# An encoder trunk on one core: the weights' sums of the FFN's block products made by adding transfers, the other sums on VectorE

## The chip, the cores and the metric

The kernel runs on one core of one Trainium2 chip. Its engines are called as in the profile: PE (TensorE matmul; PEld is its weight load), DVE (VectorE), ACT (ScalarE), POOL (GpSimd) and SP (SyncE, which only issues transfers here). The metric is the device time of one execution in microseconds, the median of three runs.

## The reference, cut to what matters

Two layers over 1024 tokens of width 1024 in float32: windowed attention in the first, a gated linear recurrence in the second, each with cross-attention into 256 memory tokens. Each layer ends with a gated FFN of width 2816 (22 blocks of 128) with a convolution of three taps along the tokens.

```python
def conv_ffn(v, w_in, conv_w, conv_b, w_out):
    gate, up = jnp.split(v @ w_in, 2, axis=-1)
    hid = jax.nn.gelu(dwconv_centred(gate, conv_w, conv_b)) * up
    return hid @ w_out
...
        h = h + rmsnorm(y, norm_g[layer, 1])
        f = conv_ffn(rmsnorm(h, norm_g[layer, 2]), ffn_w_in[layer], ffn_conv_w[layer],
                     ffn_conv_b[layer], ffn_w_out[layer])
        h = h + rmsnorm(f, norm_g[layer, 3])
```

## The kernel before

**Arithmetic.** Every float32 operand is split into two float32r parts, a high part that ACT casts and a low part, the remainder, that DVE subtracts (`split`, L83 to L85; the same in `wunit`, L73 to L75). A product is three matmuls: high by high, high by low, low by high (`mmk`, L496).

**The program.** `start` (memory keys and values, and the norm of the eight token tiles, interleaved), `window` (attention of layer 0), `WOut.finish`, `ffn` of layer 0, `hgrn`, `WOut.finish` and `ffn` of layer 1, in this order. A norm takes its reciprocal root from POOL (`rstd_of`, L91: nrs, prs), and in the attention POOL adds the two halves of the rotary embedding (L247 and L248: rq from t1 and t2), which PE then transposes (L256: ptq).

**The FFN's block products.** `ffn` (L499) multiplies 2 x 2 blocks with seven products instead of eight, by sums of operand blocks. The blocks of the first matmul are halves of the contraction, gate against up, and halves of the tokens. Its first two units (`PLAIN`) are done plainly; `operands` makes the sums of the activations meanwhile, on DVE. Then 20 units of one block of 128 hidden columns follow:

- `load` fetches the unit's weights on SP, two units ahead.
- `weights` makes four sums of 128x512 (L605, L606, L608, L612) and seven splits of 512 wide, one product's operand each. They are drawn one by one between the products of the unit before (`ahead`).
- `prod` runs a product of 12 matmuls into one of the PSUM banks X, V or Y. Between products ACT or DVE reads the partial sums out (s1, s5, su, g, u).
- `conv` does the convolution, gelu and gate: two operations of ACT and three of DVE, 1024 wide (L536 to L541).
- `hidden` makes, for each pair of units, four sums of the hidden activations of 128x512 on POOL (L655 to L658: tt) and stores seven blocks to DRAM (hd).
- `sums`, for each pair of units, loads the four weight blocks of the second matmul (L635: w), adds four times on POOL (L637 to L640) and stores the sums to DRAM (w2s).

The second half of the FFN is seven products over the tokens and 11 pairs of hidden blocks each (`SECOND`, 132 matmuls a product). `unit` loads a weight block and a hidden block and splits them. The last product (k = 4) keeps its last `LAST` pairs back and runs them token tile by token tile; after each comes `tail`: the norm, the residual, the store and, in layer 0, the norm and transposes of the next layer (`norm_T`). The other four tiles have their `tail` within the same product, after its pairs 1, 3, 5 and 7.

**What sets the order.** The lines above do not. A scheduler with a simulated timeline puts each instruction in its engine's queue as early as its model has it ready, so that work of the FFN can stand far ahead of its place in the code. Each engine's queue then runs strictly in that order. A transfer also waits for the semaphore slot that the transfer eight before it on the same kind of queue used.

Of the kernel before, what the change touches and what calls it, by code (L numbers as in the profile page):

```python
# [39 lines left out]
LAST = 3  # L40
# [4 lines left out]
def build(tc, A, out):  # L45
# [59 lines left out]
    def norm_T(pl, pst, src, g, dh, dl, t, tag="n"):  # L105
        ss = pl.tile([P, 1], F32, tag=tag + "ss", name=tag + "ss")
        u = pl.tile([P, D], F32, tag=tag + "u", name=tag + "u")
        sumsq(pl, src, ss, u)
        rs = rstd_of(pl, ss, 1, D, tag)
        dve.scalar_tensor_tensor(u, src, rs[:, 0:1], g, op0=ALU.mult, op1=ALU.mult)  # L110
        for b in range(2):
            ps = pst.tile([P, 4, P], F32, tag="pt", name="pt")
            for k in range(4):
                pe.transpose(ps[:, k, :], u[:, (4 * b + k) * P:(4 * b + k + 1) * P], ident)  # L114
            split(dh[:, 4 * b:4 * b + 4, t * P:(t + 1) * P],
                  dl[:, 4 * b:4 * b + 4, t * P:(t + 1) * P], ps)
# [224 lines left out]
    class WOut:  # L341
# [84 lines left out]
        def finish(self):  # L426
# [28 lines left out]
            self.first = wunit(A["ffw1"][l, 0, :, 1024:], pl=self.wf) if l == 0 else None  # L455
# [43 lines left out]
    def ffn(l, wo, dst, gnext, halves_, out_halves):  # L499
# [13 lines left out]
        ORDER = (1, 5, 6, 2, 7, 3, 4)  # L513
# [4 lines left out]
        half = [None, 0]  # L518

        def slot():  # L520

            if half[1] == 0:
                half[0] = [ring.tile([P, 1024], F32R, tag=t, name=t) for t in ("wh", "wl")]
            c = slice(half[1] * 512, (half[1] + 1) * 512)
            half[1] = 1 - half[1]
            return half[0][0][:, c], half[0][1][:, c]

# [5 lines left out]
        def conv(f, g, ups):  # L533
# [6 lines left out]
            for m, u in ups:  # L540
                dve.tensor_tensor(c[:, m], u, c[:, m], op=ALU.mult)  # L541
# [5 lines left out]
        def plain(f):  # L547

            wg = wo.first if f == 0 and wo.first else wunit(A["ffw1"][l, f, :, 1024:])
            wu = wunit(A["ffw1"][l, f, :, :1024])  # L550
# [6 lines left out]
            for ps, m in ((gi, ti), (gj, tj)):  # L557
                act.activation(g[:, m], ps, AF.Copy, scale=-1.0)
            return conv(f, g, ((ti, ui), (tj, uj)))

        def operands():
# [3 lines left out]
            for kk in range(2):  # L565
# [12 lines left out]
                t3, t2, t4 = tmp("w2"), tmp("c", 3), tmp("sx")  # L578
# [11 lines left out]
        def load(f):  # L590
            raw = [stg.tile([P, 1024], F32, tag="st", name="st") for _ in range(2)]
            for x, r in enumerate(raw):
                nc.sync.dma_start(r, A["ffw1"][l, f, :, x * 1024:(x + 1) * 1024])
            return raw

        def weights(raw):

            a1, a2 = raw
            L_, R_ = slice(0, 512), slice(512, 1024)
            sx = fp.tile([P, 1024], F32, tag="sx", bufs=1, name="sx")  # L600
            def op(src, neg=False):
# [4 lines left out]
            dve.tensor_tensor(sx[:, R_], a2[:, L_], a2[:, R_], op=ALU.add)  # L606
# [21 lines left out]
        w2d = dram.tile([NP2, P, 4, 512], F32, name=f"w2s{l}")  # L628
        even = [None]

        def sums(p):

            r = fp.tile([P, 4, 512], F32, tag="w2", bufs=1, name="w2")
            s3 = fp.tile([P, 512], F32, tag="s3", bufs=1, name="s3")
            nc.sync.dma_start(r, A["ffw2"][l, p])  # L635
            a11, a12, a21, a22 = (r[:, q, :] for q in range(4))
            pool.tensor_tensor(s3, a11, a21, op=ALU.add)  # L637
            pool.tensor_tensor(a21, a21, a22, op=ALU.add)  # L638
# [23 lines left out]
        def first_units():  # L662
# [10 lines left out]
            ops = [next(gen) for _ in range(7)]  # L673
# [3 lines left out]
            def start(w):  # L677

                prod(1, w, X[-1], True)
                s[1] = fp.tile([P, 512], F32, tag="s1", bufs=1, name="s1")  # L680
                act.copy(s[1], X[-1])
# [600 lines left out]
```

## Time and profile before

| | before |
|---|---|
| median of 3 runs | 2832.14 us (2828.93 to 2833.56) |
| the profiled execution | 2830.25 us, its span 2828.4 us |
| mean granted clock of TensorE | 0.977 |
| transfers | 355.12 MB, 126 GB/s over the span |

Five stages follow one another; the two FFNs take from about 596 to 1270 us and from 2137 us to the end. Times of rows are microseconds from the span's start unless marked as durations. In a row of a group, the numbers behind the bar are the busy time in us, the mean duration of one in ns, and the idle time of the engine just before them with what ended it. PE's clock is granted by a throttle, and a row of busy time by stretches shows it as a share of full speed.

### The profile page before, as it was taken

Reading aid. Unit: us, or ns where it says so; the run is one execution under the profiler, and the core shown is the slowest. Engines: PE = TensorE matmul, PEld = TensorE weight load, DVE = VectorE, ACT = ScalarE, POOL = GpSimd, SP = SyncE. Lnnn points to the kernel's source line nnn. Section 1 sums busy time; section 2 is a strip of 40 time slices with the busy share of each in tenths; the row PEclk is TensorE's granted clock in tenths of the full one; section 3 lists DMA queues with packets and bytes.
Section 4 is the critical chain, followed back from the end, with each engine's and each line's share of the span. In section 5 each row is a group of like instructions: output and inputs, shape, how many; then the busy total and the mean of one; then the engine's idle time right before and its main releaser. Section 6 shows DMA issues by size and latency. Waiting matters only on the chain.

```text
span 2828.4 us, 38853 instructions
## 1 busy us (share of the span) xinstructions
PE 2687.6 (95%) x14264; PEld 2286.9 (81%) x14264; DVE 1987.3 (70%) x3227; ACT 1376.0 (49%) x2614; POOL 641.1 (23%) x525
## 2 busy tenths in 40 slices
PE   8999989997899999997999999999898899999998
PEld 7888877886778888887898888898787777888886
DVE  6588676678876765575757778878477886776555
ACT  6367676534334444454544545545454334444443
POOL 1210120215531110021112223222212553111012
PEclk9999999998999999998999999999999899999999
DMA  7111213734553336672111111111562564323766
GB/s 280 52 42 29 60 57 99 233 120 168 199 180 105 104 119 234 193 245 92 42 53 46 46 34 49 40 41 60 155 203 94 190 229 154 112 97 133 224 193 216
DMA packets 182127, 355.12 MB, mean 126 GB/s; under 512 B 16816, under 2 KB 73520, under 8 KB 179120
## 3 DMA queue, kind: packets, MB, share of 16 engines
q1 hardware_dynamic: 179488, 348.18, 37.3%
q10 hardware_dynamic: 2448, 4.46, 0.4%
q8 instruction: 112, 1.84, 0.3%
q14 instruction: 79, 0.65, 0.1%
HBM read 257.68 MB, written 94.90 MB: 125 GB/s over the span
## 4 chain that ended last, share of the span: by engine, by line
PE 76%; DVE 9%; POOL 5%; issue 4%; DMA 3%; ACT 2%; SPq 0%; DVEq 0%; POOLq 0%; ACTq 0%
PE X L496 19%; PE V L496 12%; PE pj L79 7%; PE pj L80 7%; PE pj L81 7%; PE pb L80 3%; PE pb L79 3%; PE pb L81 3%; PE Y L496 3%; PE po L1100 1%; PE pt L308 1%; PE pa L1052 1%; DMA w<-in_ffw_dram 1%; PE pt L114 1%; POOL w L638 1%
## 5 line engine op out<-in xcount | busy, mean ns | idle before, releaser
L85 DVE TENSOR_TENSOR wl<-st,wh 128x512 fp32r<-128x512 f32 (+1 forms) x314 | 322.3, 1040 | 228.8 <-ACT wh L84 224.9
L84 ACT CAST wh<-st 128x512 fp32r<-128x512 f32 (+1 forms) x314 | 246.9, 800 | 305.4 <-PE X L496 126.4
L79 PE MATMUL pj<-wh,uh 128*128 128x256 f32 (+1 forms) x768 | 235.7, 307 | 1.0 <-DVE ul L85 0.5
L81 PE MATMUL pj<-wh,ul 128*128 128x256 f32 (+1 forms) x768 | 234.2, 305 | 0.0
L80 PE MATMUL pj<-wl,uh 128*128 128x256 f32 (+1 forms) x768 | 233.9, 305 | 0.0
L79 PE MATMUL pj<-uh,wh 128*128 128x512 f32 x512 | 205.1, 401 | 4.8 <-DVE xl L85 2.5
L80 PE MATMUL pj<-ul,wh 128*128 128x512 f32 x512 | 203.9, 398 | 0.0
L81 PE MATMUL pj<-uh,wl 128*128 128x512 f32 x512 | 203.2, 397 | 0.0
L75 DVE TENSOR_TENSOR wl<-st,wh 128x1024 fp32r<-128x1024 f32 (+1 forms) x93 | 119.1, 1287 | 46.4 <-ACT wh L74 46.2
L79 PEld LDWEIGHTS pj<-wh,uh 128*128 128x128 f32 x768 | 147.7, 192 | 3.0 <-DVE ul L85 0.9
L80 PEld LDWEIGHTS pj<-wl,uh 128*128 128x128 f32 x768 | 147.8, 193 | 1.1
L81 PEld LDWEIGHTS pj<-wh,ul 128*128 128x128 f32 x768 | 147.6, 192 | 0.5
L1046 POOL TENSOR_TENSOR E<-EP,q 128x256 f32<-128x256 f32 x64 | 51.3, 801 | 414.5 <-DVE EP L1039 386.0
L74 ACT CAST wh<-st 128x1024 fp32r<-128x1024 f32 (+1 forms) x103 | 104.0, 1016 | 79.7 <-PE pj L80 42.8
L496 PE MATMUL V<-uh,wh 128*128 128x512 f32 x344 | 135.5, 394 | 4.5 <-ACT wh L84 4.5
L496 PE MATMUL V<-uh,wl 128*128 128x512 f32 x344 | 135.7, 394 | 3.4 <-DVE wl L85 3.4
L496 PE MATMUL X<-wh,wl 128*128 128x512 f32 x352 | 137.0, 390 | 0.0
L496 PE MATMUL X<-wl,wh 128*128 128x512 f32 x352 | 136.8, 389 | 0.0
L496 PE MATMUL X<-wh 128*128 128x512 f32 x352 | 136.4, 389 | 0.0
L496 PE MATMUL V<-ul,wh 128*128 128x512 f32 x344 | 135.3, 393 | 0.0
L79 PEld LDWEIGHTS pj<-uh,wh 128*128 128x128 f32 x512 | 96.8, 189 | 24.0 <-DVE xl L85 2.9
L81 PEld LDWEIGHTS pj<-uh,wl 128*128 128x128 f32 x512 | 96.8, 189 | 19.8
(365 smaller groups left out, 7813.8 us busy)
## 6 DMA issues: line engine op xcount, KB each, us to landing
st<-in_ffw_dram SPq DMA_DIRECT2D x88, 512.0 KB, 4.2
st<-hid SPq DMA_DIRECT2D x154, 256.0 KB, 4.2
w<-in_ffw_dram SPq DMA_DIRECT2D x22, 1024.0 KB, 5.0
hid<-tt SPq DMA_DIRECT2D x88, 256.0 KB, 2.1
st<-w2s SPq DMA_DIRECT2D x88, 256.0 KB, 4.0
w2s<-w SPq DMA_DIRECT2D x22, 768.0 KB, 3.3
hid<-c SPq DMA_DIRECT2D x66, 256.0 KB, 2.5
st<-in_ffw_dram SPq DMA_DIRECT2D x66, 256.0 KB, 3.8
```

The costliest lines, as they stand in the source:

```text
L74: act.copy(h[:, :n], raw)
L75: (eng or dve).tensor_tensor(l[:, :n], raw, h[:, :n].bitcast(F32), op=ALU.subtract)
L79: pe.matmul(o, ah, bh, start=first, stop=False)
L80: pe.matmul(o, ah, bl, start=False, stop=False)
L81: pe.matmul(o, al, bh, start=False, stop=last)
L84: act.copy(h, src)
L85: dve.tensor_tensor(l, src, h.bitcast(F32), op=ALU.subtract)
L114: pe.transpose(ps[:, k, :], u[:, (4 * b + k) * P:(4 * b + k + 1) * P], ident)
L308: pe.transpose(tp[:, j, :], sm[:, j, c * P:(c + 1) * P], ident)
L496: pe.matmul(o, x, y, start=new, stop=e, skip_group_check=not first)
L638: pool.tensor_tensor(a21, a21, a22, op=ALU.add)
L1046: pool.tensor_tensor(gl, pl_, ql, op=ALU.mult)
```

## The change

Four things are done.

1. The sums of the first matmul's weights: `load` fetches blocks into two more tiles (sx, sy) and adds to them by three transfers that POOL issues with `accum_op` (the sum of source and destination is written to the destination). `weights` only splits: three operands of 1024, two products' each, and one of 512. The order of the products becomes 2, 5, 6, 7, 3, the next unit's 1, and 4, and ACT copies g and, in the plain units, u out of PSUM.
2. The sums of the second matmul's weights: `sums` makes them inside DRAM by six transfers of POOL, three copies and three that add.
3. The four sums in `hidden` move from POOL to DVE.
4. The second half: the first four tails move from the last product to the one before (k = 2), with the transposes kept for the last; `LAST` is 7 in layer 0 and 10 in layer 1, and a new pool holds 5 and 8 of those operands.

The weight arrays are laid out to match. The core of the diff:

```diff
-LAST = 3
+LAST = (7, 10)
+HOLD = (5, 8)
...
-    def norm_T(pl, pst, src, g, dh, dl, t, tag="n"):
+    def norm_T(pl, pst, src, g, dh, dl, t, tag="n", ub=2, halt=False):
...
-        u = pl.tile([P, D], F32, tag=tag + "u", name=tag + "u")
+        u = pl.tile([P, D], F32, tag=tag + "u", bufs=ub, name=tag + "u")
...
+        def turn(pst):
+            for b in range(2):
...
+        if halt:
+            return turn
+        turn(pst)
...
-            for ps, m in ((gi, ti), (gj, tj)):
-                act.activation(g[:, m], ps, AF.Copy, scale=-1.0)
-            return conv(f, g, ((ti, ui), (tj, uj)))
+            u = fp.tile([P, T], F32, tag="u", bufs=1, name="u")
+            for gp, up_, m in ((gi, ui, ti), (gj, uj, tj)):
+                act.activation(g[:, m], gp, AF.Copy, scale=-1.0)
+                act.copy(u[:, m], up_)
+            return conv(f, g, u)
...
-                t3, t2, t4 = tmp("w2"), tmp("c", 3), tmp("sx")
+                t3, t2, t4 = tmp("sy", 2), tmp("c", 3), tmp("sx", 2)
...
         def load(f):
-            raw = [stg.tile([P, 1024], F32, tag="st", name="st") for _ in range(2)]
-            for x, r in enumerate(raw):
-                nc.sync.dma_start(r, A["ffw1"][l, f, :, x * 1024:(x + 1) * 1024])
-            return raw
+            w = A["ffw1"][l, f]
+            a1 = stg.tile([P, 1024], F32, tag="st", name="st")
+            a22 = stg.tile([P, 1024], F32, tag="st", name="st")[:, :512]
+            sx, sy = [fp.tile([P, 1024], F32, tag=t, bufs=2, name=t) for t in ("sx", "sy")]
+            nc.sync.dma_start(a1, w[:, 1024:])
+            for c in range(2):
+                nc.sync.dma_start(sx[:, c * 512:(c + 1) * 512], w[:, :512])
+            nc.sync.dma_start(sy, w[:, 1024:])
+            nc.sync.dma_start(a22, w[:, 512:1024])
+            pool.dma_start(sx, w[:, 512:1536], accum_op=ALU.add, max_dma_last_dim=8192)
+            pool.dma_start(sy[:, :512], sx[:, :512], accum_op=ALU.add, max_dma_last_dim=8192)
+            pool.dma_start(sy[:, 512:], sy[:, :512], accum_op=ALU.add, max_dma_last_dim=8192)
+            return a1, sx, sy, a22
         def weights(raw):
-            a1, a2 = raw
-            L_, R_ = slice(0, 512), slice(512, 1024)
-            sx = fp.tile([P, 1024], F32, tag="sx", bufs=1, name="sx")
-            def op(src, neg=False):
-                h, l_ = slot()
-                (nsplit if neg else split)(h, l_, src)
-                return h, l_
-            dve.tensor_tensor(sx[:, L_], a1[:, L_], a2[:, L_], op=ALU.add)
-            dve.tensor_tensor(sx[:, R_], a2[:, L_], a2[:, R_], op=ALU.add)
-            yield op(a1[:, L_])
-            dve.tensor_tensor(a1[:, L_], sx[:, R_], a1[:, L_], op=ALU.add)
-            yield op(sx[:, R_])
-            yield op(a1[:, L_])
-            s4 = fp.tile([P, 512], F32, tag="s4", bufs=1, name="s4")
-            dve.tensor_tensor(s4, a1[:, L_], a1[:, R_], op=ALU.add)
-            yield op(a1[:, R_])
-            yield op(sx[:, L_])
-            yield op(s4)
-            yield op(a2[:, R_])
+            for src in raw:
+                n = src.shape[-1]
+                h, l_ = [ring.tile([P, 1024], F32R, tag=t, name=t)[:, :n] for t in ("wh", "wl")]
+                split(h, l_, src)
+                yield h, l_
+        def operand(units, k):
+            u, c = {1: (0, 0), 2: (0, 1), 5: (1, 0), 7: (1, 1), 6: (2, 0), 3: (2, 1), 4: (3, 0)}[k]
+            return tuple(x[:, c * 512:(c + 1) * 512] for x in units[u])
...
-        w2d = dram.tile([NP2, P, 4, 512], F32, name=f"w2s{l}")
...
         def sums(p):
-            r = fp.tile([P, 4, 512], F32, tag="w2", bufs=1, name="w2")
-            s3 = fp.tile([P, 512], F32, tag="s3", bufs=1, name="s3")
-            nc.sync.dma_start(r, A["ffw2"][l, p])
-            a11, a12, a21, a22 = (r[:, q, :] for q in range(4))
-            pool.tensor_tensor(s3, a11, a21, op=ALU.add)
-            pool.tensor_tensor(a21, a21, a22, op=ALU.add)
-            pool.tensor_tensor(a11, a11, a21, op=ALU.add)
-            pool.tensor_tensor(a12, a12, a11, op=ALU.add)
-            nc.sync.dma_start(w2d[p][:, 0:3, :], r[:, 0:3, :])
-            nc.sync.dma_start(w2d[p][:, 3, :], s3)
+            w, o = A["ffw2"][l, p], w2d[p]
+            for c in range(2):
+                pool.dma_start(o[c], w[0])
+            pool.dma_start(o[2:4], w[2:4])
+            pool.dma_start(o[0:2], w[1:3], accum_op=ALU.add, max_dma_last_dim=8192)
+            pool.dma_start(o[2], o[0], accum_op=ALU.add, max_dma_last_dim=8192)
+            pool.dma_start(o[3], o[2], accum_op=ALU.add, max_dma_last_dim=8192)
...
-            pool.tensor_tensor(t1[:, lo], e[:, oi], e[:, oj], op=ALU.subtract)
-            pool.tensor_tensor(t1[:, hi], c[:, oj], e[:, oj], op=ALU.subtract)
-            pool.tensor_tensor(t2[:, lo], t1[:, hi], e[:, oi], op=ALU.add)
-            pool.tensor_tensor(t2[:, hi], t2[:, lo], c[:, oi], op=ALU.subtract)
+            dve.tensor_tensor(t1[:, lo], e[:, oi], e[:, oj], op=ALU.subtract)
+            dve.tensor_tensor(t1[:, hi], c[:, oj], e[:, oj], op=ALU.subtract)
+            dve.tensor_tensor(t2[:, lo], t1[:, hi], e[:, oi], op=ALU.add)
+            dve.tensor_tensor(t2[:, hi], t2[:, lo], c[:, oi], op=ALU.subtract)
...
-                w = dict(zip(ORDER, ops))
-                ahead()
-                prod(5, w[5], v, True)
-                s5 = fp.tile([P, 512], F32, tag="s5", bufs=1, name="s5")
-                act.copy(s5, v)
-                ahead()
-                prod(6, w[6], x, False)
-                su = fp.tile([P, 512], F32, tag="su", bufs=1, name="su")
-                act.copy(su, x)
-                ahead()
-                prod(2, w[2], y, True)
+                w = lambda k: operand(ops, k)
+                prod(2, w(2), y, True)
                 u = fp.tile([P, T], F32, tag="u", bufs=1, name="u")
                 dve.tensor_tensor(u[:, ti], y, s[1], op=ALU.add)
                 ahead()
-                prod(7, w[7], x, False)
+                prod(5, w(5), v, True)
+                s5 = fp.tile([P, 512], F32, tag="s5", bufs=1, name="s5")
+                act.copy(s5, v)
+                prod(6, w(6), x, False)
+                su = fp.tile([P, 512], F32, tag="su", bufs=1, name="su")
+                act.copy(su, x)
+                prod(7, w(7), x, False)
                 g = gtile()
-                dve.tensor_tensor(g[:, tj], x, s5, op=ALU.add)
+                act.copy(g[:, tj], x)
+                dve.tensor_tensor(g[:, tj], g[:, tj], s5, op=ALU.add)
                 ahead()
...
-            h, l_ = [ring.tile([P, 1024], F32R, tag=t, name=t) for t in ("wh", "wl")]
+            pl = hold_pool if k == 4 and 0 <= p - (NP2 - LAST[l]) < HOLD[l] else ring
+            h, l_ = [pl.tile([P, 1024], F32R, tag=t, name=t) for t in ("wh", "wl")]
...
-            if todo and len(made) < 3:
+            if todo and len(made) < (LAST[l] if todo[0][0] == 4 else 3):
...
+        hold_pool = tc.alloc_tile_pool(name=f"fh{l}", bufs=HOLD[l], reuse_waits="tile")
...
-                norm_T(np_, pst, x, g0, uh, ul, 4 * b + t)
+                return norm_T(np_, pst, x, g0, uh, ul, 4 * b + t, ub=4, halt=True)
...
-                if k == 4 and p in (1, 3, 5, 7):
-                    t = p // 2
-                    tail(ib, t, y["c12"][:, t, :], ss["q12"][:, t:t + 1], y["c22"][:, t, :], ss["q22"][:, t:t + 1])
+                if k == 2 and p in (2, 4, 6, 8):
+                    t = p // 2 - 1
+                    turns.append(tail(ib, t, y["c12"][:, t, :], ss["q12"][:, t:t + 1],
+                                      y["c22"][:, t, :], ss["q22"][:, t:t + 1]))
+                if k == 4 and gnext and p < 4:
+                    turns.pop(0)(pst)
```

The order of instructions moves in two places. **POOL, the start of the program.** Here stand the reciprocal roots of the norms (nrs) and the first rotary sums of the attention (rq); w2s is the DRAM tensor of the second weights' sums. Before:

```order
L63 MEMSET nhalf 128x8
L91 ISA
L91 TENSOR_TENSOR nrs<-nms,nhalf 128x1 x2
L75 TENSOR_TENSOR wl<-st,wh 128x1024
L91 TENSOR_TENSOR nrs<-nms,nhalf 128x1 x8
L247 TENSOR_TENSOR rq<-t_832,t_833 128x320
L248 TENSOR_TENSOR rq<-t_832,t_833 128x64
```

Now, with what each waits for, first around the first nrs and then up to the first rq:

```order
L633 DMA w2s_6544<-in_ffw_dram 16x4096 [waits DMASW7_49]
L633 DMA w2s_6544<-in_ffw_dram 16x4096 [waits DMASW0_49]
L93 TENSOR_TENSOR nrs<-nms,nhalf 128x1 [waits DVE_49,Pool_49]
L634 DMA w2s_6544<-in_ffw_dram 16x8192 [waits DMASW1_49]
L633 DMA w2s_6544<-in_ffw_dram 16x4096 [waits DMASW2_49]
L93 TENSOR_TENSOR nrs<-nms,nhalf 128x1 [waits DVE_49]
```

```order
L637 DMA w2s_20143<-w2s_20143 32x2048 [waits DMASW0_49]
L637 DMA w2s_20143<-w2s_20143 32x2048 [waits DMASW1_49]
L637 DMA w2s_20143<-w2s_20143 32x2048 [waits DMASW2_49]
L254 TENSOR_TENSOR rq<-t_832,t_833 128x320 [waits DMAHW2_49,DMAHW1_49,DMAHW4_49,DVE_49,Activation_49]
L255 TENSOR_TENSOR rq<-t_832,t_833 128x64
```

All 132 transfers of `sums`, of both layers (w2s_6544 and w2s_20143), now stand here: 17 of them ahead of the first nrs, 89 ahead of the tenth and 131 ahead of the first rq. Each from the ninth on waits for the slot of the one eight before it (DMASW0 to DMASW7). Before, the sums stood on POOL and SP within the FFN.

**DVE, one unit of the FFN's first half.** wl is the low part of a split; c, g and u are the tiles of the convolution, tt the hidden sums. Before, then now:

```order
L605 TENSOR_TENSOR sx<-st 128x512
L606 TENSOR_TENSOR sx<-st 128x512
L85 TENSOR_TENSOR wl<-st,wh 128x512 x2
L608 TENSOR_TENSOR st<-sx,st 128x512
L612 TENSOR_TENSOR s_9022<-st 128x512
L85 TENSOR_TENSOR wl<-sx,wh 128x512
L85 TENSOR_TENSOR wl<-st,wh 128x512
L537 SCALAR_TENSOR_TENSOR c<-g,ncw,c 128x1023
L538 SCALAR_TENSOR_TENSOR c<-g,ncw,c 128x1023
```

```order
L87 TENSOR_TENSOR wl<-st,wh 128x512
L87 TENSOR_TENSOR wl<-st,wh 128x1024
L533 SCALAR_TENSOR_TENSOR c<-g,ncw,c 128x1023
L534 SCALAR_TENSOR_TENSOR c<-g,ncw,c 128x1023
L87 TENSOR_TENSOR wl<-sx,wh 128x1024
L536 TENSOR_TENSOR c<-u,c 128x1024
L651 TENSOR_TENSOR tt<-c 128x512
L695 TENSOR_TENSOR u<-Y,s_9449 128x512
L709 TENSOR_TENSOR u<-V,su 128x512
L652 TENSOR_TENSOR tt<-tt,c 128x512
L87 TENSOR_TENSOR wl<-sy,wh 128x1024
```

The four sums of 512 are gone, the splits are wider and fewer, and the hidden sums (L651, L652) stand among them.

More of the change, by code (lines that the diff above doesn't have):

```diff
@@ L110, in norm_T @@
         dve.scalar_tensor_tensor(u, src, rs[:, 0:1], g, op0=ALU.mult, op1=ALU.mult)
[L111 to L116, printed above, removed]
+        def turn(pst):
+            for b in range(2):
+                ps = pst.tile([P, 4, P], F32, tag="pt", name="pt")
+                for k in range(4):
+                    pe.transpose(ps[:, k, :], u[:, (4 * b + k) * P:(4 * b + k + 1) * P], ident)
+                split(dh[:, 4 * b:4 * b + 4, t * P:(t + 1) * P],
+                      dl[:, 4 * b:4 * b + 4, t * P:(t + 1) * P], ps)
+        if halt:
+            return turn
+        turn(pst)
     kvd = [dram.tile([4, P, 2, 256], F32, name=f"kvd{l}") for l in range(2)]
@@ L547, in plain @@
         def plain(f):
-            wg = wo.first if f == 0 and wo.first else wunit(A["ffw1"][l, f, :, 1024:])
-            wu = wunit(A["ffw1"][l, f, :, :1024])
+            wg = wo.first if f == 0 and wo.first else wunit(A["ffw1"][l, f, :, :1024])
+            wu = wunit(A["ffw1"][l, f, :, 1024:])
             bank = lambda t: psx.tile([P, 512], F32, tag=t, name=t)
@@ L672, in first_units, with start @@
             gen = weights(raws.pop(PLAIN))
-            ops = [next(gen) for _ in range(7)]
+            ops = list(gen)
             X = [psx.tile([P, 512], F32, tag="X", name="X")]
             s = {}
-            def start(w):
-                prod(1, w, X[-1], True)
+            def start(units):
+                prod(1, operand(units, 1), X[-1], True)
                 s[1] = fp.tile([P, 512], F32, tag="s1", bufs=1, name="s1")
                 act.copy(s[1], X[-1])
-            start(ops[0])
+            start(ops)
             yield
@@ L719, in first_units @@
                     X.append(psx.tile([P, 512], F32, tag="X", name="X"))
-                    start(nxt[0])
-                prod(4, w[4], x, False)
+                    start(nxt)
+                prod(4, w(4), x, False)
                 act.copy(g[:, ti], x)
                 ahead()
-                hidden(f, conv(f, g, ((slice(0, T), u),)))
+                hidden(f, conv(f, g, u))
                 if f % 2 == 1:
@@ L819, in ffn @@
                 second_ahead()
-                if k == 4 and p >= NP2 - LAST:
+                if k == 4 and p >= NP2 - LAST[l]:
                     hold.append((p, h, l_))
```

33 lines of the change are left out of this document (14 added, 19 removed).

## The prediction

> **What bounds the kernel now.** I read the page first, then the chain of waits, then busy time by stretches, and last the start of the program on POOL and PE.
>
> ```profile
> span 2828.4 us, 38853 instructions
> PE 2687.6 (95%) x14264; PEld 2286.9 (81%) x14264; DVE 1987.3 (70%) x3227; ACT 1376.0 (49%) x2614; POOL 641.1 (23%) x525
> ```
>
> PE is busy for 95% of the span, so a saving off PE counts only where PE stands still. The profiled execution took 2830.25 us (its span and 1.85 us around it), 0.07% under the median of 2832.14; the sum is made against 2830.25.
>
> The change lies in the two FFN stages and, by the order of POOL's instructions, at the very start. The chain and PE's first matmuls of a stage mark what the first half of each FFN takes:
>
> ```profile
> 596.42 0.48 PE L496 MATMUL X<-uh,xwh 128*128 128x512 f32 x1
> 825.50 2.72 PE V L496 x12
> 1060.20 32.95 PE X L496 x144
> 2137.15 0.48 PE L496 MATMUL X<-uh,wh 128*128 128x512 f32 x1
> 2602.23 32.98 PE X L496 x144
> ```
>
> A block product is 12 matmuls in 2.72 us. Twenty units of seven products are 380.8 us, and two plain units of 96 matmuls 43.5: 424.3 us undisturbed. The rows of 144 begin with the last product of the half, which ends 2.72 us on. So the halves last 1062.9 - 596.4 = 466.5 and 2604.9 - 2137.2 = 467.8 us, an **excess of 85.7 us** in both. Busy time by stretches (columns: PE, PEld, DVE, ACT, POOL with counts, granted clock, DMA share, GB/s) shows where:
>
> ```profile
> 640.00:680.00 40.00, 23.64 (x87) 18.17 (x86) 38.29 (x39) 15.61 (x23) 28.23 (x11) 0.79 0.45 162
> 700.00:820.00 120.00, 106.15 (x446) 85.91 (x445) 92.18 (x91) 42.82 (x69) 62.20 (x38) 0.94 0.58 203
> 860.00:1040.00 180.00, 180.00 (x796) 149.03 (x795) 127.88 (x163) 79.11 (x123) 26.61 (x19) 1.00 0.30 101
> 2180.00:2220.00 40.00, 23.51 (x83) 18.16 (x82) 39.52 (x39) 16.95 (x23) 27.48 (x10) 0.74 0.42 147
> 2260.00:2360.00 100.00, 86.10 (x360) 69.95 (x359) 79.50 (x76) 34.53 (x54) 55.48 (x34) 0.93 0.62 220
> 1260.00:1300.00 40.00, 25.52 (x118) 20.97 (x118) 31.20 (x52) 20.03 (x35) 7.84 (x13) 0.75 0.64 222
> 2800.00:2829.00 29.00, 14.72 (x65) 11.84 (x64) 11.96 (x23) 4.86 (x10) 2.54 (x4) 0.84 0.30 110
> ```
>
> PE idles 16.4 and 16.5 us while the operand sums fill DVE (640 to 680, 2180 to 2220), and 13.9 and 13.9 us while POOL makes the second weights' sums (700 to 820, 2260 to 2360): 60.6 us. The other 25 us of the excess go with the lower granted clock (0.74 to 0.94) after such gaps. From 860 to 1040 PE never waits; nothing is to be won there. The ends of the two stages hold another 14.5 and 14.3 us.
>
> **The FFN half, term by term.** In the second kind of gap DVE works longer at the same operations. First 700 to 820, then 860 to 1040, and POOL in the first:
>
> ```profile
> L606 DVE TENSOR_TENSOR sx<-st 128x512 f32<-128x512 f32 x6 | 6.3, 1043 | 0.0
> L538 DVE SCALAR_TENSOR_TENSOR c<-g,ncw,c 128x1023 f32<-128x1023 f32 x5 | 9.4, 1873 | 0.1
> ...
> L606 DVE TENSOR_TENSOR sx<-st 128x512 f32<-128x512 f32 x9 | 6.2, 685 | 0.0
> L538 DVE SCALAR_TENSOR_TENSOR c<-g,ncw,c 128x1023 f32<-128x1023 f32 x10 | 12.8, 1280 | 0.2
> ...
> L638 POOL TENSOR_TENSOR w<-w 128x512 f32<-128x512 f32 x7 | 12.3, 1754 | 0.3
> ```
>
> A sum of 512 takes DVE 1.04 us beside POOL's sums and 0.69 without. The change takes all sums of this half from POOL, so this cause goes. DVE also loses four weight sums a unit (4 x 0.69 = 2.8 us) and gets, every second unit, the four hidden sums (1.4 us a unit).
>
> ```profile
> L85 DVE TENSOR_TENSOR wl<-st,wh 128x1024 fp32r<-128x1024 f32 x132 | 171.2, 1306 | 125.4 <-ACT wh L84 123.8 <-DMA st<-in_ffw_dram 1.1
> L84 ACT CAST wh<-st 128x1024 fp32r<-128x1024 f32 x132 | 138.4, 1053 | 177.4 <-PE X L496 78.5 <-PE V L496 68.7 <-DMA st<-hid 22.2
> L84 ACT CAST wh<-st 128x512 fp32r<-128x512 f32 x182 | 108.5, 616 | 127.9 <-PE X L496 47.9 <-PE V L496 28.3 <-PE Y L496 22.9
> ```
>
> Seven splits of 512 become three of 1024 and one of 512. On ACT that is 7 x 0.62 = 4.3 against 3 x 1.05 + 0.62 = 3.8 us, eaten by the new copy of g (about 0.6). On DVE it is about 7 x 0.7 = 4.9 against 3 x 1.31 + 0.7 = 4.6. Together DVE does some 1.7 us less in a unit that now costs it 127.9 / 180 x 19.04 = 13.5 us. I count the 27.8 us of the second kind of gap as gone with its share of the clock loss (27.8 / 60.6 x 25 = 11.5): 39 us. In the first kind DVE stays full with the operand sums, which the change leaves, and takes on hidden sums; two waits of PE for DVE's product with Y do go, as ACT now copies both halves out of PSUM:
>
> ```profile
> PE Y L496 <- DVE c L541: 24.9, 2, 13.5
> ```
>
> But PE then only reaches the first unit's operands earlier, which DVE still owes. I take a third of 32.9 + 13.5, that is 15 us. What stands late next there is DVE.
>
> The second halves run at 29.92 us a product, PE without gaps, and stay. The change brings the first tails forward to the product before the last and holds 7 and 10 pairs for the end instead of 3. What ends last in the program is a late load of x, behind two stores:
>
> ```profile
> 2818.22 1.74 SPq L782 DMA_DIRECT2D x<-h1d  x2
> 2822.04 0.75 DVE L788 SCALAR_TENSOR_TENSOR x<-c,prs,x 128x512 f32<-128x512 f32 x1 [3.79 <-DMA x<-h1d]
> ```
>
> The wider spacing of the four last tails (30 matmuls, 6.8 us, instead of 9, 2.0 us) covers this load: about 7 us there and 5 at the end of the first FFN. **Gain in all: 39 + 15 + 12 = 66 us**; bounds 20 (half of the contended gaps alone) and 114 (the whole excess and both ends, 85.7 + 28.8).
>
> The first weights' sums now go as three dependent adding transfers a unit on POOL's queue, each waiting for the one before. The nearest rows:
>
> ```profile
> st<-in_ffw_dram SPq DMA_DIRECT2D x88, 512.0 KB, 4.2
> hid<-tt SPq DMA_DIRECT2D x88, 256.0 KB, 2.1
> w<-in_ffw_dram SPq DMA_DIRECT2D x22, 1024.0 KB, 5.0
> ```
>
> At 2.1 to 4.2 us each, three take 6 to 13 us of the unit's 19.04, and sx and sy are two deep, so I cost them at nothing. The cover is gone above 6.3 us a transfer; then each further microsecond costs 3 x 40 = 120 us. Bounds: 0 and, at 7 us, 80.
>
> **The start.** The order shows all 132 transfers of the second weights' sums, of both layers, on POOL's queue ahead of the first rotary sum rq, with the ten rstd powers of the start among them. From the ninth on each waits for the one eight before it. So POOL gets to the first rq only when 123 of them have landed. Now:
>
> ```profile
> 54.99 0.55 POOL L91 TENSOR_TENSOR nrs<-nms,nhalf 128x1 f32<-128x1 f32 x1 [5.40 <-DVE nms L89]
> 77.20 0.86 POOL L247 TENSOR_TENSOR rq<-t,t 128x320 f32<-128x320 f32 x1 [21.66 <-DVE t L246]
> 79.79 0.87 POOL L247 TENSOR_TENSOR rq<-t,t 128x320 f32<-128x320 f32 x1 [1.00 <-DVE t L246]
> 85.85 0.87 POOL L247 TENSOR_TENSOR rq<-t,t 128x320 f32<-128x320 f32 x1 [4.90 <-DVE t L246]
> 90.01 0.88 POOL L247 TENSOR_TENSOR rq<-t,t 128x320 f32<-128x320 f32 x1 [3.00 <-DVE t L246]
> 78.11 0.33 PE L256 MATMUL ptq<-ident,rq 128*128 128x128 f32 x1 [1.96 <-POOL rq L247]
> ```
>
> PE needs rq for its transposes, t is one buffer deep and the projection's bank two, so PE, DVE and ACT all stop behind POOL after some three tiles. As those tiles are ready then, some 4 us come back (2.6 between the first two rq, 4.2 and more later). Bytes up to then: 22 pairs x 1.049 MB copied = 23.1 MB; of the same amount added, eight transfers of 0.26 MB may still fly: 21.0 MB. SP's own loads of this stage come from the first of these rows, 0.264 x 80 = 21.1 MB:
>
> ```profile
> 0.00:80.00 80.00, 67.30 (x421) 61.76 (x422) 50.82 (x66) 47.08 (x76) 12.06 (x19) 0.99 0.76 264
> 10.00:20.00 10.00, 8.37 (x48) 7.46 (x48) 8.20 (x11) 8.78 (x15) 4.62 (x4) 1.00 1.03 413
> ```
>
> The second shows all 16 DMA engines full (share 1.03) at 413 GB/s. Lower end: each byte once at that rate, 65.2 / 0.413 = 158 us. Upper end: a copy inside DRAM counts as read and write, an adding one as two reads and a write, (46.1 + 63.0 + 21.1) / 0.413 = 315 us. No transfer inside DRAM stands in the trace. I take 245, a little over the middle: a load that reads DRAM and a store that writes it are apart in the rows, and such a transfer has to do both, though perhaps at once. The first rq then comes at 245 instead of 77.2: 245 - 77 - 4 = **164 us lost**; bounds 77 and 234. Nothing hides it, since the attention behind it needs every rq.
>
> The Trainium skill, "DMA: Bandwidth & Descriptors", section "Latency and other measured facts", gives 207 to 214 GB/s per direction for copies between HBM tensors; no run here shows it yet. Its estimate for 44.1 MB at 210 and 21.1 at 413 is 261 us, a loss of 180 and 2944 us in all.
>
> **Sum**: 2830.25 + 164 - 66 = 2928 us.
>
> **The rivals.**
> - *The transfers hide behind the start.* The order was laid out as if they did. At some 4 us from issue to landing, as the load rows have it, 132 transfers eight deep take 132 x 4 / 8 = 66 us, under 77; nothing is lost, and the time is 2830 - 66 = 2764, faster. It decides at a first rq before 77 + 4 + 66 = 147 us. Against it: this needs 44 MB in 66 us beside 21 MB of SP's, 990 GB/s, against 413 with the engines full. For it: the gain may be larger than I took. Chance 0.16. The Trainium skill, "DMA: Bandwidth & Descriptors", section "Anatomy of one DMA — SWDGE (gpsimd) path", gives an estimate of 2.0 us plus bytes at 436 GB/s for each transfer; 132 x 2.8 / 8 = 46 us would hide them too; the 413 of the row speaks against adding eight such rates.
> - *DRAM to DRAM at the full rate of loads.* First rq at 158: 2830 + 77 - 66 = 2841. It needs a second read to cost nothing. Chance 0.14, of which 0.03 falls within 0.2% and 0.03 below.
> - *Adding transfers slower than a read and a write apiece*: at the start past 315 us, or in the FFN past 6.3 us each. 2830 + 234 - 66 = 2998 and up to 80 more. Chance 0.17.
>
> **How the numbers follow.** The forecast, a first rq between some 180 and 315 us, has 0.53. About 0.2% (5.7 us) is what a measurement of this kernel can tell from no change. Faster: 0.16 + 0.03 = 0.19; within: 0.03; slower: 0.53 + 0.08 + 0.17 = 0.78. The low end joins the lower loss with the upper gain, 2830 + 77 - 114 = 2793; the high end the upper loss with the lower gain, 3044, rounded to 3050. Outside lie most of the first rival and the top of the last, 0.2.
>
> **What would show it.** Right: in the profile after, the first rq at 180 to 315 us, PE idle before it, POOL's queue full of transfers that wait for each other, DMA high through that stretch; both FFN first halves near 435 to 440 us, sums of 512 on DVE at 0.69 us throughout; the end under 8 us behind PE's last matmul. Wrong: a first rq before 147 us, or first halves as long as now, with PE waiting for splits that wait for adding transfers.

## The result and the profile after

| | before | after |
|---|---|---|
| median | 2831.26 us (4 runs, 2828.93 to 2833.56) | 2933.32 us (4 runs, 2932.32 to 2935.85) |
| ratio | | 1.0362, 95% interval 1.0344 to 1.0380 |
| span of the profiled execution | 2828.4 us | 2931.4 us |
| mean granted clock | 0.977 | 0.968 |

The kernel became 102 us slower; 2928 had been forecast. The page after, its span and busy times:

```profile
span 2931.4 us, 39076 instructions
PE 2692.7 (92%) x14264; PEld 2288.0 (78%) x14264; DVE 1828.9 (62%) x3031; ACT 1391.3 (47%) x2542; POOL 522.2 (18%) x601
```

DVE is busy 158 us less and POOL 119 us less, as the change intended; PE has the same work to do and 103 us more in which to do it. The marks that the prediction used split these 103 us. First, the start on POOL: the last transfer that stands ahead of the first rotary sum, and that sum.

```profile
217.51 0.77 POOL L637 DMA_DIRECT2D w2s<-w2s  x1 [1.01 <-DMA w2s<-w2s]
231.87 0.85 POOL L254 TENSOR_TENSOR rq<-t,t 128x320 f32<-128x320 f32 x1 [13.59 <-DVE t L253]
```

The first rq comes at 231.9 in place of 77.2 us, 154.7 us later; the forecast was 245. Next, PE's first matmul of each FFN and the last of each first half.

```profile
752.17 0.48 PE L503 MATMUL X<-uh,xwh 128*128 128x512 f32 x1
1194.81 0.39 PE L503 MATMUL X<-u4h,wl 128*128 128x512 f32 x1
2268.61 0.48 PE L503 MATMUL X<-uh,wh 128*128 128x512 f32 x1
2714.01 0.39 PE L503 MATMUL X<-u4h,wl 128*128 128x512 f32 x1
```

The halves take 442.6 and 445.4 us, against 466.4 and 467.7 between the same two marks before (these marks lie 0.1 us inside the ends used ahead). Laid end to end:

| stretch | predicted | measured |
|---|---|---|
| program start to first FFN | +164 | 752.2 - 596.4 = +155.8 |
| the two first halves | -54 (39 + 15) | -23.8 - 22.3 = -46.1 |
| end of the first half of FFN 0 to FFN 1 | -5 | 1073.8 - 1074.3 = -0.5 |
| end of the first half of FFN 1 to the program's end | -7 | 217.4 - 223.5 = -6.1 |
| sum | +98 | +103.1 |

What the halves still lose against 424.3 us shows in PE's waits, first for 752 to 1195 and then for 2268 to 2714 us (in total, times, longest):

```profile
PE V L503 <- ACT wh L86: 7.9, 1, 7.9
PE X L503 <- ACT wh L86: 2.6, 2, 2.3
...
PE V L503 <- ACT wh L86: 11.3, 1, 11.3
PE X L503 <- ACT wh L86: 2.2, 1, 2.2
```

Before, in the two halves, DVE was the one waited for:

```profile
PE X L496 <- DVE g L713: 13.8, 5, 6.5
PE Y L496 <- DVE c L541: 11.4, 1, 11.4
...
PE X L496 <- DVE g L713: 14.7, 4, 6.8
PE Y L496 <- DVE c L541: 13.5, 1, 13.5
```

Now it is ACT's cast of the weights of the first block-product unit, and the chain of waits tells what ACT waited for:

```profile
793.66 1.15 DVE u4l L87
794.83 0.33 SPq L595
795.15 0.05 issue
795.21 4.27 DMA sx<-in_ffw_dram
...
807.88 2.72 DMA sx<-in_ffw_dram
810.60 6.79 DMA sy<-sy
817.39 0.03 ACTq L86
```

The last operand sum leaves the tile sx at 794.8; only then may `load` fill it, and a load and three adding transfers follow one another until 817.4, 22.6 us with PE idle for some ten of them. Behind this unit PE has no wait above 1.4 us in either half, and DVE's sums of 512 are short throughout (840 to 1190 us, one row of four):

```profile
L651 DVE TENSOR_TENSOR tt<-c 128x512 f32<-128x512 f32 x9 | 6.2, 693 | 0.3
```

### The profile page after: what moved, and what is told of

It reads as the page before. It is cut to its first block, busy times and chain, and to the rows that moved or that the text cites. A ratio compares the mean times of both kernels' runs of the same rounds, so it can differ in the third digit from the quotient of the medians.

```text
span 2931.4 us, 39076 instructions
## 1 busy us (share of the span) xinstructions
PE 2692.7 (92%) x14264; PEld 2288.0 (78%) x14264; DVE 1828.9 (62%) x3031; ACT 1391.3 (47%) x2542; POOL 522.2 (18%) x601
## 4 chain that ended last, share of the span: by engine, by line
PE 78%; DVE 8%; DMA 8%; issue 2%; ACT 2%; POOL 1%; SPq 0%; POOLq 0%; DVEq 0%; ACTq 0%
PE X L503 22%; PE V L503 12%; PE pj L81 7%; PE pj L82 7%; PE pj L83 7%; PE Y L503 4%; PE pb L81 3%; PE pb L82 3%; PE pb L83 3%; DMA st<-in_wmk_dram 3%; DMA kvd<-vm 1%; PE po L1102 1%; DMA x<-in_x_dram 1%; PE pt L315 1%; PE pa L1054 1%
## 5 line engine op out<-in xcount | busy, mean ns | idle before, releaser
L87 DVE TENSOR_TENSOR wl<-st,wh 128x1024 fp32r<-128x1024 f32 (+1 forms) x234 | 259.2, 1112 | 329.1 <-ACT wh L86 318.7
L86 ACT CAST wh<-st 128x1024 fp32r<-128x1024 f32 (+1 forms) x234 | 218.4, 937 | 275.6 <-PE X L503 135.4
L77 DVE TENSOR_TENSOR wl<-st,wh 128x1024 fp32r<-128x1024 f32 (+1 forms) x93 | 119.5, 1291 | 115.0 <-ACT wh L76 114.8
L76 ACT CAST wh<-st 128x1024 fp32r<-128x1024 f32 (+1 forms) x103 | 103.9, 1015 | 125.9 <-DMA st<-in_wmk_dram 47.0
L117 PE MATMUL pt<-ident,nu 128*128 128x128 f32 x272 | 41.7, 301 | 91.6 <-DVE nu L112 65.2
## 6 DMA issues: line engine op xcount, KB each, us to landing
w2s<-in_ffw_dram POOLq DMA_DIRECT2D x44, 512.0 KB, 11.8
```

The lines of the kernel that those rows point to most:

```text
L76: act.copy(h[:, :n], raw)
L77: (eng or dve).tensor_tensor(l[:, :n], raw, h[:, :n].bitcast(F32), op=ALU.subtract)
L86: act.copy(h, src)
L87: dve.tensor_tensor(l, src, h.bitcast(F32), op=ALU.subtract)
```

## The experiments

Each is told against the kernel that it was made from. e10 leaves out the sums of the second weights; all others compute the whole. "FFN start" and "halves" are read from the same marks of PE as above.

| run | median us | ratio to before | FFN 0 starts | halves |
|---|---|---|---|---|
| before | 2829 to 2831 | | 596.4 | 466.4, 467.7 |
| the change | 2933.32 | 1.0362 (1.0344 to 1.0380) | 752.2 | 442.6, 445.4 |
| e1_sums_in_ffn | 2878.17 | 1.0180 (1.0148 to 1.0212) | 598.3 | 494.8, 492.4 |
| e2_sums_spread | 2782.40 | 0.9838 (0.9821 to 0.9854) | 599.5 | 443.6, 444.8 |
| e3_before_sums_dram | 2928.19 (one run) | | 753.1 | 437.0, 438.7 |
| e4_rq_on_dve | 2840.23 (one run) | | 666.0 | 438.7, 445.2 |
| e5_first_sums_early | 2755.09 | 0.9740 (0.9725 to 0.9754) | 600.8 | 429.3, 432.8 |
| e6_before_spread_tails | 2769.90 | 0.9793 (0.9776 to 0.9809) | 599.3 | 436.4, 438.9 |
| e7_hidden_on_pool | 2793.16 (one run) | | 599.3 | 447.2, 452.7 |
| e8_small_packets | 2792.63 (one run) | | 614.0 | 441.2, 446.6 |
| e9_after_small_packets | 2925.51 (one run) | | 744.7 | 442.2, 445.9 |
| e10_after_copies | 2887.92 (one run) | | 709.5 | 442.8, 444.8 |

### e1: the transfers where the code has them

`mark[0]` is the last adding transfer that `load` issued.

```diff
-                pool.dma_start(o[c], w[0])
+        with tc.issue_after(mark[0].ins):
+            for c in range(2):
+                pool.dma_start(o[c], w[0])
...
```

> The changed kernel with the 132 transfers of the second weights' sums queued on POOL behind the adding transfers of the FFN units in whose code they stand, so that none is left at the start. Theory 'the start is the whole loss': the first rq is back near 77 us and the time falls by the 154 us that the first rq came late, 2933 - 154 = 2779 us, with FFN first halves of 443 to 446 us as now. Rival 'the transfers have to be paid somewhere': in the first halves the DMA engines are already 0.72 busy; a pair's chain of three dependent adding transfers at 10 to 12 us each holds POOL's queue for some 30 of the 38 us of two units, and the adding transfers of load stand behind it; the halves grow past 480 us each and the time is 2850 us or more.

2878 us: the start is back (FFN 0 at 598.3), but each half grows by some 50 us, and the rival is right. PE's, ACT's and POOL's waits in the first half:

```profile
PE X L503 <- ACT g L706: 35.7, 8, 6.7
...
ACT wh L86 <- DMA sx<-in_ffw_dram: 29.9, 4, 9.1
...
POOL w2s L636 <- DMA w2s<-in_ffw_dram: 50.8, 10, 6.8
```

POOL's queue stands behind a pair's chain, the adding transfers of the next unit behind POOL, ACT's cast behind them, and in ACT's own queue the copy of g that frees PE's bank.

### e2: the transfers spread over stages that load little

```diff
-        for f in range(PLAIN // 2):
-            sums(f)
+        sums()
...
+            for n, (d, x, kw) in enumerate(moves):
+                with tc.issue_after(marks[l][n * len(marks[l]) // len(moves)].ins):
+                    pool.dma_start(d, x, **kw)
```

`marks[0]` are the 32 second rotary sums, `marks[1]` POOL's products of the recurrent stage.

> The changed kernel with the same 132 transfers spread out: those of layer 0 two at a time behind the rotary sums of the window stage, those of layer 1 one at a time behind POOL's products of the recurrent stage, pipelined so that an adding transfer comes a step after what it adds to. Theory 'the start is the whole loss': first rq near 77 us, 2933 - 154 = 2779 us, and 2764 to 2790 us with what the later rotary sums wait. Rival 'the transfers cost where they stand, for bandwidth': the window stage and the recurrent stage, which load at 30 to 65 GB/s, get longer by some tens of us, 2800 to 2860 us.

2782 us, as the first theory had it: the same transfers cost 3 us up to the first FFN and at most 2 behind it, and the change turns from 3.6% slower to 1.6% faster than before.

### e3: the kernel before with this part alone

The edit is `sums` of the change with its layout of the weights, put into the kernel before.

> The kernel before with the new sums of the second weights alone (six transfers a pair inside DRAM, wherever the scheduler puts them) and the weights laid out for them; all else as before. Theory 'the start is the whole loss, the other parts only gain': the first rq comes at about 232 us and the time is 2831 + 154 = 2985 us, less what the FFN gains as POOL's sums there go (up to 28 us), so 2957 to 2985 us. Rival 'the other parts of the change lose as well': the loss of this part alone is near the 102 us of the whole change, 2933 us or less.

2928 us. The start loses what it loses in the whole change (FFN 0 at 753.1), but the halves, 437.0 and 438.7 us, are better than those of the whole change. My expected gain of 28 us was too small: taking four sums of 512 a pair off POOL, with the loads and stores that belong to them, gains 58 us in the two halves. The literal range of the rival fits the time, and in part its reason too: the rest of the change loses 5.6 and 6.7 us in the halves and wins 6.7 at the end. Stretches from the first FFN's start, 44 to 64 and 104 to 224 us on:

```profile
797.05:817.05 20.00, 12.13 (x44) 9.46 (x43) 19.73 (x21) 10.41 (x14) 6.17 (x4) 0.74 0.25 80
857.05:977.05 120.00, 120.00 (x531) 99.34 (x531) 86.15 (x109) 51.24 (x82) 19.21 (x13) 1.00 0.30 106
```

The gap of 13.9 us in the second stretch is gone altogether, with hidden sums still on POOL; of 16.4 us in the operand sums 7.9 are left, at which DVE is the one waited for. DVE's sum of 512 takes 841 ns in the second stretch, against 1043 in the gap before and 685 where nothing disturbed it:

```profile
L606 DVE TENSOR_TENSOR sx<-st 128x512 f32<-128x512 f32 x7 | 5.9, 841 | 0.0
```

e3 takes out POOL's sums and their transfers together. That it was the sums is read from these times and from PE's waits for DVE; no run parts the two.

### e4 and e8: which wait holds the start

e4 puts all 132 transfers in one block behind the tenth reciprocal root and makes on DVE what POOL did of the projection:

```diff
-                    pool.tensor_tensor(rq[:, :320], t1, t2, op=ALU.add)
+                    dve.tensor_tensor(rq[:, :320], t1, t2, op=ALU.add)
...
+            with tc.issue_after(roots[9].ins):
```

> The changed kernel with nothing of the attention left behind the transfers on POOL: all 132 stand in one block behind the tenth reciprocal root of the start, and the rotary sums and the low parts of the projection's weights are made on DVE. The transfers still run while the window stage begins. Theory 'queue': the loss is rq's place behind the transfers in POOL's queue; it goes, and the time is 2779 us and up to 25 us more for the 32 rotary sums on DVE, 2780 to 2805 us. Theory 'bandwidth': the full DMA engines starve SP's loads of the stage, wherever rq is made; PE waits for the projection's weights, and 50 us or more of the loss stay, 2830 to 2930 us.

2840 us, in the range of 'bandwidth': with nothing of the attention left on POOL, FFN 0 still starts 70 us later than before: the first rq comes at 137.2 us, as DVE waits for the small loads cos and sin. DMA issues of 55 to 260 us (KB, median us to landing):

```profile
kvd<-vm SPq DMA_DIRECT2D x2, 256.0 KB, 44.9
...
sin<-in_sin_dram SPq DMA_DIRECT2D x1, 256.0 KB, 48.7
...
cos<-in_cos_dram SPq DMA_DIRECT2D x1, 128.0 KB, 47.9
```

Before, sin took 3.9 us from issue to landing, kvd 2.7 and cos 2.8. e8 changes one thing in e4:

```diff
-                pool.dma_start(o[0:2], w[1:3], accum_op=ALU.add, max_dma_last_dim=8192)
+                pool.dma_start(o[0:2], w[1:3], accum_op=ALU.add, max_dma_last_dim=2048)
```

and likewise for the other five transfers. By the packets in the traces the rows of the adding transfers go from 8 to 2 KB and those of the copies from 16 and 32 to 4 KB; the expectation below has them as 8 and 16 KB cut to 2.

> e4_rq_on_dve with every transfer of the second weights' sums cut to rows of 2 KB in place of 8 and 16 KB. In e4 one load, sin, landed 48.7 us after its issue beside the block of transfers, and that was most of the 68 us that the first FFN started late. Theory 'long rows are served whole, so a load waits behind many of them': sin lands in 10 to 20 us and 30 us or more come back, 2790 to 2812 us. Rival 'bytes': the DMA engines are full either way, the load waits as long, 2830 to 2860 us.

2793 us, in the range of the theory. The first rq comes at 91.9 us, and 52 of the 70 us come back:

```profile
kvd<-vm SPq DMA_DIRECT2D x2, 256.0 KB, 14.8
...
sin<-in_sin_dram SPq DMA_DIRECT2D x1, 256.0 KB, 19.0
```

The bytes are the same and the engines as full (share 1.00 to 1.04 in e4 and 1.01 to 1.10 in e8, from 80 to 240 us), so what starves the loads is the length of the rows beside them. The Trainium skill, "DMA: Bandwidth & Descriptors", section "Queues, rings and completion order", says that a DMA engine alternates between queues and drains a whole packet before it switches; these two runs agree with that.

### e9: short rows in the change itself

The edit of e8 in the changed kernel, POOL's order untouched.

> The changed kernel, POOL's order and all else as it is, with every transfer of the second weights' sums cut to rows of 2 KB. Theory 'two causes, queue first': POOL still reaches the first rq only when nearly all transfers have landed, and their bytes are the same, so the first rq stays at 215 to 235 us and the time at 2915 to 2935 us, though the loads of the start land in 10 to 20 us in place of 40 to 46. Rival 'starved loads alone': the start's norms and projections come earlier and with them the first rq, by 30 us or more; 2900 us or less.

2926 us, 8 us less, as expected of 'queue first'. But the run also corrects my picture of the change. Here DVE has t ready at 196 us, and rq waits for POOL alone:

```profile
195.53 0.49 DVE L253 TENSOR_TENSOR t<-pj,sin 128x320 f32<-128x320 f32 x1 [1.50 <-DMA sin<-in_sin_dram]
...
226.39 1.15 POOL L254 TENSOR_TENSOR rq<-t,t 128x320 f32<-128x320 f32 x1
```

In the changed kernel it is the other way round: POOL is free at 218.3 us, and rq waits 13.59 us more for t (row above), which waits for a load:

```profile
230.62 0.49 DVE L252 TENSOR_TENSOR t<-pj,cos 128x320 f32<-128x320 f32 x1 [44.84 <-DMA cos<-in_cos_dram]
```

cos was issued at 193.9 us only and landed 36.7 us later. The chain of waits of this stretch, its longest pieces, is a chain of loads; its last one, sk, lands beside cos:

```profile
9.49 45.95 DMA st<-in_wmk_dram
...
80.31 40.64 DMA st<-in_wmk_dram
...
123.68 28.10 DMA x<-in_x_dram
...
174.03 39.98 DMA kvd<-vm
214.03 17.88 DMA sk<-in_a_sink_dram
```

So two waits of nearly the same length stand side by side, POOL's queue (218 to 226 us) and the starved loads (232 us). Short rows alone (e9) leave the queue, and the first rq gains 5.5 us. The reciprocal roots stand in that queue too: DVE waits 61.7 us in all for them in e9, and 0.5 in the change, where the loads come later still. e4 took rq out of the queue, with the transfers also behind the last root, and the loads left 70 of the 156 us.

### e10: what the adding costs

The changed kernel with `accum_op` taken out of the three adding transfers of a pair.

> The changed kernel with the three adding transfers of each pair as plain copies of the same size and order; the sums of the second weights are left out, so only the times count. It prices the adding. Theory of the prediction 'a copy is a read and a write, an adding transfer two reads and a write': the adding half of the bytes falls from three shares to two, the whole from 130 to 109 MB (46.1 + 42.0 + 21.1), and the first rq comes at 0.84 of 232 us, 190 to 200 us, the time 2895 us. Rival 'an adding transfer costs no more than a copy': first rq at 225 to 235 us, 2925 to 2935 us.

2888 us, and the first rq at 189.5, just under its range: the first theory. In the last stretch with full engines POOL's queue moves copies inside DRAM alone in e10 (160 to 180 us) and adding transfers inside DRAM alone in the changed kernel (200 to 220 us). Its rows there (packets, MB, share of the 16 engines):

```profile
q0 software_dynamic: 978, 5.42, 73.3%
...
q0 software_dynamic: 672, 3.67, 88.6%
```

Copies run at 5.42 MB / (20 us x 0.733) = 370 GB/s of full engines and adding transfers at 3.67 / (20 x 0.886) = 207. Against loads (413 at a share of 1.03, so 401) a byte copied costs 1.08 and a byte added 1.94; the bounds of the prediction had been 1 for both, and 2 and 3. The single packets agree: one of 8 KB takes 628 ns where it adds and 309 where it copies (medians over the two traces). By these prices the bytes up to the first rq are an estimated (23.1 x 1.08 + 21.0 x 1.94 + 21.1) MB / 401 GB/s = 216 us, and POOL is free at 218.3. The copies' rate is not the 207 to 214 GB/s that the Trainium skill, "DMA: Bandwidth & Descriptors", section "Latency and other measured facts", gives for copies between HBM tensors in tiles of 128 rows of 16 KiB; for the transfers here the measurement decides.

### e5: the new wait at the first unit

e2 with sx and sy of units 2 and 3 made early in DRAM by the same spread transfers, and loaded whole:

```diff
+            if f in early:
+                nc.sync.dma_start(a22, w[:, 512:1024])
+                nc.sync.dma_start(sx, early[f][0])
+                nc.sync.dma_start(sy, early[f][1])
+                return a1, sx, sy, a22
```

> e2_sums_spread with the first weights' sums of units 2 and 3 of each layer made early as well, in DRAM, by the same spread transfers, so that load fetches sx and sy of these two units by plain loads; all later units keep the chain of three adding transfers. Theory 'new wait': what is left of the excess in the first halves (443.6 and 444.8 us against 424.3) is the first unit's chain of adding transfers, which starts only when the operand sums free sx and sy and takes 22.6 us in the profile; PE's waits for ACT's wh (11.0 and 13.6 us) fall to 3 us or less with their dent in the clock, the halves to 430 to 435 us, the time from 2782 to 2760-2768 us. Rival 'DVE owes the operands anyway': the waits pass from wh to DVE's products, the halves stay above 440 us and the time within 5 us of 2782.

2755 us. The first theory holds, and 27 us come back from two units a layer, 5 more than its range had. PE's waits in the halves, of e2 and then of e5 (its first half has no wait for wh):

```profile
PE V L504 <- ACT wh L86: 7.6, 1, 7.6
PE X L504 <- ACT wh L86: 3.4, 1, 3.4
...
PE V L504 <- ACT wh L86: 10.5, 1, 10.5
PE X L504 <- ACT wh L86: 3.1, 1, 3.1
```

```profile
PE V L504 <- ACT wh L86: 3.0, 1, 3.0
```

This is the fastest version of the study, 2.6% under the kernel before.

### e6 and e7: the sums on DVE

e6 is the kernel before with e2's spread transfers and the new second half.

> The kernel before with two parts of the change alone: the second weights' sums as transfers in DRAM, spread as in e2_sums_spread, and the new second half (earlier tails, more pairs held). The first weights' sums stay on DVE and the hidden sums on POOL. Theory 'POOL's sums of the second weights were the whole cost': first halves of 437 to 439 us as in e3_before_sums_dram, ends as in the changed kernel, 2829 - 58 - 7 = 2764 us, some 18 us under e2_sums_spread; the adding transfers of load then cost more than they save. Rival 'taking sums off DVE pays': halves of 445 us or more, 2785 us or more.

2770 us, 12.5 under e2: the first theory, with halves of 436.4 and 438.9 us. As it stands in the change, the new first half (adding transfers of `load`, hidden sums on DVE) costs more than it saves; with the first unit's chain out of the way (e5) it saves 15.

e7 is e2 with `pool` in place of `dve` in the four hidden sums.

> e2_sums_spread with the four hidden sums of a pair back on POOL. Theory of the prediction 'all sums of POOL beside DVE lengthen DVE's': DVE's operations beside them take up to half as long again for 7 of each 38 us, PE waits again, 10 us or more on the halves, 2790 us or more. Rival 'DVE has slack': DVE is busy 0.59 of the first half and PE does not wait for it; the halves stay within 2 us, 2778 to 2786 us.

2793 us, 11 more, the size that the prediction's theory named, but not by its way. DVE's operations do get longer in part (a split of 512 takes 1278 ns for 692 in e2), but PE does not wait for them. PE's waits grow at the first unit alone (11.0 for 7.6 and 15.7 for 10.5 us), and two rows of POOL show a cause in the first layer:

```profile
643.27 5.49 POOL L658 TENSOR_TENSOR tt<-c 128x512 f32<-128x512 f32 x1 [37.64 <-DVE g L572]
648.71 0.90 POOL L599 DMA_DIRECT2D sx<-in_ffw_dram  x1
```

The first hidden sum takes 5.49 us beside DVE's operand sums and stands ahead of the first adding transfer in POOL's queue; this transfer is issued 1.8 us later than in e2. In the second layer the sum takes 6.58 us, and there SP's queue passes the delay on: the store of the sum stands ahead of the load of sx, which is issued at 2172.4 us in place of 2166.1. Later units show no wait of PE above 1.4 us.

## Why the prediction was right, and where not

The time (2928 against 2933) and the side came out, and the forecast's case is the one that happened; its parts less exactly. That the sum came within 5 us is luck: 8 us too much loss at the start stood against 13 too much gain in the FFNs.

- **The start, 164 predicted, 154.7 at the first rq and 155.8 at the first FFN.** That transfers hoisted ahead of rq would hold it was shown: e2 moves them and the loss is gone. The price, "a little over the middle" of 158 and 315 us, was a choice between two bounds and came out too high: e10 shows that an adding transfer costs about two loads a byte (1.94) but a copy hardly more than one (1.08), so that "such a transfer has to do both" shows in the price of the adding ones alone. With the measured prices the queue is an estimated 216 us long, not 245. Two more things were not in the step, and the first of them brought the time back towards the forecast. "So POOL gets to the first rq only when 123 of them have landed" is true at 218 us, but is not what ended the wait: loads that landed after 18 to 46 us instead of 3 to 7 did, 13.6 us later. The prediction counted SP's bytes, not what long rows do to loads on another queue; e4 and e8 measure that at 52 us where POOL's queue is out of the way. And the 4 us that ready tiles were to give back did not come: the fifth rq is 154.1 us late and the first 154.7.
- **"A third of 32.9 + 13.5, that is 15 us" and the 39 us of contention: 54 predicted, 46.1 measured.** The contended gaps went with POOL's four sums of the second weights, as e3 shows by itself: 58 us with no other part of the change, more than the 54. The rest of the change then takes 12 us away again in the halves. "What stands late next there is DVE" failed: it is the first unit's weights.
- **"So I cost them at nothing"** is the step that was wrong. The estimate looked at the steady state, where it holds: 18.3 us of landings (8.6 + 4.2 + 5.5) fit into 19.04 us a unit, and PE does not wait. At the first unit nothing runs ahead, since the operand sums hold sx and sy, and the whole chain lies bare: the halves took 442.6 and 445.4 us where the prediction wanted to see 435 to 440. e5 prices it at 27 us over both layers, 14.2 + 12.0 in the halves.
- **The hidden sums on DVE** were counted as a part of the same cause; e7 gives them about 11 us, of which 8.6 are longer waits of PE at the first unit.
- **The tails: 12 predicted, 6.6 measured.** At the program's end the 7 us came (6.1). The 5 us at the end of the first FFN did not (0.5): PE's transposes there wait for DVE's splits instead of the norm. Before, then after:

```profile
PE pt L114 <- DVE nu L110: 7.1, 2, 5.3
PE pt L114 <- DVE nms L89: 6.2, 1, 6.2
...
PE pt L117 <- DVE ul L87: 11.7, 6, 5.7
```

- **Rivals.** The transfers did not hide (first rq before 147 us), nor go at the rate of loads (158; the copies nearly did, the adding ones did not), nor pass 315 us. The first rival's time, 2764, is not reached by placing the transfers elsewhere alone (e2, 2782); e5 and e6 come near it with further edits.

What stays open: the reciprocal roots stayed on POOL in every run, so what the starved loads alone would cost with all transfers at the very start was not tried. That copies cost 1.08 and adding transfers 1.94 of a load was measured, not explained. Of the 70 us of e4, 18 are left in e8, and no run takes them apart.

## What to carry to other kernels

A transfer that is ready at once is not free at once: a scheduler that sees only its inputs may pull it ahead of work that needs the same queue and the same DMA engines, so look at where the queue has it and pin it to a stage whose DMA share is low. A chain of dependent transfers that hides in the steady state lies bare at the first turn of the loop; check what holds its buffers there. When a wait is undone and little comes back, look for a second one of the same length beside it.

## What the hardware showed beyond the expected

- Small loads from SP (kvd, cos, sin) beside transfers with rows of 8 to 32 KB took 44.9 to 48.7 us from issue to landing; beside the same transfers in rows of 2 and 4 KB, 14.8 to 19.0 us, with the DMA engines as full.
- With eight in flight on full engines, transfers inside DRAM took 10.7 to 11.8 us each to land; spread out (e2), 3.4 to 5.2 us.
- POOL took 5.49 and 6.58 us (e7) and 10.07 us (the kernel before) for one sum of 128x512 beside DVE's operand sums, where 1.3 to 1.6 us is its mean for such sums in e3's undisturbed stretch.
- A packet of 8 KB inside DRAM took 628 ns where it adds (the change) and 309 where it copies (e10).
